# Two-layer hybrid backbone on one core: static buffer rings, a per-feature-tile start for the latent tokens, and modulation vectors spread one per step

## The chip, the cores and the metric

The kernel runs on one core of a Trainium2 chip. The metric is device time in microseconds (us) of one execution, as a median over runs. Five engines work side by side, each through its own list of instructions in order: TensorE (PE, matrix products into PSUM), VectorE (DVE), ScalarE (ACT), GpSimd (POOL) and SyncE (SP, which issues the DMAs). They wait for one another through semaphores.

## What is computed

Two layers of a backbone with 512 latent tokens and 256 context tokens, width 1024, batch 1. The reference, cut to what matters:

```python
def _layer(x, ctx, mod_x, mod_c, lp, rope, update_ctx):
    shift_x, scale_x, gate_x = jnp.split(mod_x[:, None, :], 3, axis=-1)
    shift_c, scale_c, gate_c = jnp.split(mod_c, 3, axis=-1)
    hx = _rms_norm(x, lp['norm_w']) * (1 + scale_x) + shift_x
    hc = _rms_norm(ctx, lp['norm_w']) * (1 + scale_c) + shift_c
    px = _project_stream(hx, lp, rope, True)          # hx @ w_in, split into the branches' parts
    pc = _project_stream(hc, lp, None, update_ctx)
    ya = _dense_attention(...)                        # MLA: latent attention
    yb = _window_attention(...)                       # SWA: window of 128, context, sink
    yc = _dense_attention(...)                        # AXA: axial rope, grouped heads
    yd_x, yd_c = _rglru_branch(...)                   # LRU: gated linear scan in both directions
    x = x + gate_x * _merge_branches((ya, yb, yc, yd_x), px['gate'], px['merge'], lp)
    if update_ctx:
        ctx = ctx + gate_c * _merge_branches(..., pc['gate'], pc['merge'], lp)
    return x, ctx

def _merge_branches(branches, z_gate, z_merge, lp):
    y = jnp.stack(branches, axis=2) * jax.nn.silu(z_gate.reshape(b, n, N_BRANCH, BRANCH_W))
    proj = jnp.einsum('bnkw,kwd->bnkd', y, lp['w_branch'])
    mix = jnp.sum(jax.nn.sigmoid(z_merge.reshape(b, n, N_BRANCH, D_MODEL)) * proj, axis=2)
    return mix @ lp['w_out']

# mod_x = silu(c) @ w_mod[l] + b_mod[l] ; mod_c = silu(c_ctx) @ w_mod[l] + b_mod[l]
```

The modulation vectors (shift, scale and gate, 1024 features each) exist for two conditions: the latent tokens' (condition 0) and the context's (condition 1).

## The kernel before

Activations stand feature by feature: a feature tile is 128 features (partitions) by 768 tokens, the 512 latent ones first. Every operand of a product is split into a high and a low part, and `mm3` (lines 161 to 165) issues three matmuls for each product. Weights come in slots of 128 by 512: `wload` (line 152) issues the DMA into `wraw`, ACT writes the high part `whi` (line 157), POOL the low part `wlo` (line 158). `fgemm` (line 312) makes feature-major products (PSUM tiles `fg`), `tgemm` (line 329) token-major ones for two token tiles (PSUM tiles `tg`). All of it is written as a trace of steps; a scheduler with a timeline of its own then orders the instructions on every engine and places the pools' buffers, so the order on an engine is not that of the source.

**The start.** SP loads the latent x and the first layer's modulation weights (`wmp`, 16 loads of 512 KB, line 180). DVE sums the squares (line 277), PE and POOL make the norm's factor and spread it over the partitions (`rb`, line 292). `scale_pe` (line 190) makes the scales of two feature tiles on PE; `shift2` (line 211) the shift of one feature: condition 0 on DVE (line 213), condition 1 on POOL (product, line 215) and ACT (sum, line 216). `make_hx` (line 298) then writes the normed, modulated feature tile `hx` as a high and a low part: line 302 on DVE, line 304 on ACT, line 305 on DVE. The first product, group `skv` (keys and values of SWA), follows `hx` tile by tile; group `sq` (its queries) comes after it. Then the context's tiles are normed, and the third token pair (context) is projected.

A unit of `gqa_prep` (line 402) is one such product of two token tiles with its tail: values are split (line 399), keys and queries normed and rotated by `head_norm` (line 344: DVE lines 352, 354, 367, 368, 369; POOL lines 341, 342, 365, 366), then transposed by PE and split again (lines 420, 421, 432 to 436).

**The layer.** After SWA's six units and its two gates come SWA's twelve attention pairs (`attn_pair`, line 474; each begins with a row maximum `nm`, line 489, on DVE), with AXA's six units and gates spread between them; then the merge of SWA (m1), AXA's attention with MLA's parts, m2, MLA's attention, the linear recurrence (`lru_scan`, line 726) with the merge of MLA (m3) beside it, the LRU gates `gl`, the merge of LRU (m4) and the output projection (`outproj`, line 836). A merge is eight steps, each with a product `fg`, a tanh on ACT (`mt`, line 812), a branch product `pj`, the product of both on DVE (line 820) and the sum on POOL (line 825). In m4 the sum is also split (`mh` on ACT, line 830, `ml` on DVE, line 831).

**Modulation vectors.** `modvec` (line 247) makes one vector of 128 features: a DMA of 512 KB into `wm`, one multiply-and-sum on DVE for each condition (line 255; the full product goes to a PSUM scrap tile or back into `wm`), then the bias (line 258), and for a scale the gain (line 226) or for a gate a factor 0.25 (line 263). Two calls of `extra()` end each step of m4 and of the output projection, and each takes one vector from a list. In layer 0 that list is filled at m4, with 24 vectors: its own eight gates and the sixteen shifts and scales of layer 1. In layer 1 there are eight, for one condition.

```python
extra()
extra()
if not first:
    pool.tensor_tensor(out=a[:, :N], in0=a[:, :N], in1=t[:, :N], op=ALU.add)
```

## Time and profile before

| | us |
|---|---|
| median of 3 runs | 1443.93 |
| lowest and highest | 1441.81, 1447.64 |
| profiled execution, span (the page gives no other time of that execution) | 1442.5 |
| PE busy | 1358.6 (94%) |
| DVE busy | 916.0 (64%) |
| POOL busy | 733.7 (51%) |
| ACT busy | 672.1 (47%) |

The profile divides one execution by engine, by line and by stretch of time. Its busy time of PE counts a matmul from its issue to its modelled end, and a matmul at the lower of the two clocks as busy for longer, so that idle time and granted clock are read together. A mean granted clock of 1.00 in a stretch is the full 2.4 GHz, 0.50 would be 1.2 GHz throughout.

### The profile page before, as it was taken

What the parts mean: (1) busy time and instruction counts of PE and PEld (TensorE: products, weight loads), DVE (VectorE), ACT (ScalarE), POOL (GpSimd) and SP (SyncE); (2) the same over time, 40 slices, a digit from 0 to 9 for tenths busy, and PEclk for the clock granted to TensorE, in tenths of its full rate; (3) what the DMA queues carried; (4) which work ended last, traced back from release to release, by engine and by line L of the source; (5) the groups of instructions that cost most, each with busy time, mean ns of one, the idle gap of its engine ahead of it and who ended that gap; (6) DMA issues with size and microseconds to landing.
All of it is one profiled execution on the core that took longest, in us unless ns stands there. A gap on an engine that the chain in (4) does not pass through costs nothing. (4 is left out here: it accounts for less than half of the span.)

```text
span 1442.5 us, 22051 instructions
## 1 busy us (share of the span) xinstructions
PE 1358.6 (94%) x8216; PEld 1195.3 (83%) x8216; DVE 916.0 (64%) x1526; ACT 672.1 (47%) x1413; POOL 733.7 (51%) x699
## 2 busy tenths in 40 slices
PE   6699989999999999999978999999999999988998
PEld 4598979899988898888867888999898778876787
DVE  5877875447746755473998367886577476458621
ACT  4445555445545444662222244556455454466231
POOL 4563623223535625675555456554345565468863
PEclk9799999999999999999989999999999999998999
DMA  9021101111111212122453442111221212322534
GB/s 358 29 60 45 40 25 45 52 44 40 46 45 36 61 36 77 52 81 76 167 172 128 155 153 67 52 49 60 67 61 39 73 45 72 98 73 73 162 112 142
DMA packets 58747, 117.82 MB, mean 82 GB/s; under 512 B 6544, under 2 KB 10640, under 8 KB 58640
## 3 DMA queue, kind: packets, MB, share of 16 engines
q1 hardware_dynamic: 58640, 116.42, 25.7%
q8 instruction: 64, 1.05, 0.3%
q14 instruction: 43, 0.35, 0.1%
HBM read 112.20 MB, written 4.19 MB: 81 GB/s over the span
## 5 line engine op out<-in xcount | busy, mean ns | idle before, releaser
L158 POOL TENSOR_TENSOR wlo<-wraw,whi 128x512 fp32r<-128x512 f32 (+2 forms) x298 | 410.4, 1382 | 361.1 <-ACT whi L157 319.6
L163 PE MATMUL fg<-hx,whi 128*128 128x512 f32 x960 | 349.7, 366 | 18.2 <-ACT mt L812 8.8
L164 PE MATMUL fg<-hx,wlo 128*128 128x512 f32 x960 | 348.2, 363 | 8.5 <-POOL wlo L158 8.5
L165 PE MATMUL fg<-hx,whi 128*128 128x512 f32 x960 | 347.1, 362 | 0.0
L157 ACT ACTIVATE whi<-wraw 128x512 fp32r<-128x512 f32 (+2 forms) x298 | 184.7, 621 | 249.3 <-DMA wraw<-in_wall_dram 153.2
L163 PEld LDWEIGHTS fg<-hx,whi 128*128 128x128 f32 x960 | 184.9, 193 | 47.0 <-ACT mt L812 9.8
L164 PEld LDWEIGHTS fg<-hx,wlo 128*128 128x128 f32 x960 | 185.1, 193 | 37.1 <-POOL wlo L158 11.7
L165 PEld LDWEIGHTS fg<-hx,whi 128*128 128x128 f32 x960 | 184.6, 192 | 25.0
L164 PE MATMUL tg<-whi,hx 128*128 128x256 f32 (+1 forms) x528 | 152.1, 290 | 7.5 <-DVE hx L305 7.5
L163 PE MATMUL tg<-whi,hx 128*128 128x256 f32 (+1 forms) x528 | 151.2, 291 | 6.5 <-ACT hx L304 6.4
L165 PE MATMUL tg<-wlo,hx 128*128 128x256 f32 (+1 forms) x528 | 151.0, 289 | 0.6 <-POOL wlo L158 0.5
L523 DVE TENSOR_TENSOR PT<-ptr,PT 128x512 fp32r<-128x512 f32 (+1 forms) x148 | 97.7, 671 | 53.8 <-ACT PT L522 52.4
L496 ACT ACTIVATE P<-s,nm 128x768 f32<-128x768 f32 (+3 forms) x120 | 91.9, 771 | 62.4 <-DVE nm L491 30.5
L522 ACT ACTIVATE PT<-ptr 128x512 fp32r<-128x512 f32 (+1 forms) x148 | 84.2, 584 | 72.9 <-PE ptr L520 67.7
L825 POOL TENSOR_TENSOR acc<-acc,mt 128x768 f32<-128x768 f32 (+1 forms) x48 | 90.1, 1879 | 47.4 <-DVE mt L820 46.4
L164 PEld LDWEIGHTS tg<-whi,hx 128*128 128x128 f32 x528 | 103.6, 197 | 10.1 <-DVE hx L305 9.4
L489 DVE TENSOR_REDUCE nm<-s 128x2 f32<-128x1536 f32 (+3 forms) x60 | 85.9, 1432 | 40.1 <-PE s L165 18.6
L163 PEld LDWEIGHTS tg<-whi,hx 128*128 128x128 f32 x528 | 103.2, 197 | 9.4 <-ACT hx L304 7.4
L165 PEld LDWEIGHTS tg<-wlo,hx 128*128 128x128 f32 x528 | 103.4, 197 | 1.1 <-POOL wlo L158 1.0
L812 ACT ACTIVATE mt<-fg 128x512 f32<-128x512 f32 x96 | 50.1, 522 | 71.9 <-PE fg L165 67.7
L510 DVE TENSOR_SCALAR P<-P,den 128x768 f32<-128x768 f32 (+3 forms) x120 | 80.2, 708 | 2.0
L519 PE MATMUL ptr<-ident,P 128*128 128x128 f32 x288 | 72.1, 278 | 1.8 <-DVE mt L820 1.8
(283 smaller groups left out, 2850.0 us busy)
## 6 DMA issues: line engine op xcount, KB each, us to landing
wraw<-in_wall_dram SPq DMA_DIRECT2D x282, 256.0 KB, 2.6
wm<-in_wmod_dram SPq DMA_DIRECT2D x32, 512.0 KB, 3.2
wmp<-in_wmod_dram SPq DMA_DIRECT2D x16, 512.0 KB, 9.1
x<-in_xT_dram SPq DMA_DIRECT2D x4, 512.0 KB, 6.0
xs<-xn SPq DMA_DIRECT2D x4, 512.0 KB, 3.8
xr<-xs SPq DMA_DIRECT2D x8, 256.0 KB, 2.8
out_dram<-xn SPq DMA_DIRECT2D x4, 512.0 KB, 3.7
wraw<-in_wall_dram SPq DMA_DIRECT2D x8, 160.0 KB, 2.2
```

Of the source, the lines that this page charges most:

```text
L157: act.activation(out=hi[:, :n], in_=raw, func=AF.Copy)
L158: pool.tensor_tensor(out=lo[:, :n], in0=raw, in1=hi[:, :n].bitcast(F32), op=ALU.subtract)
L163: pe.matmul(out=o, lhsT=a[0], rhs=b[0], start=first, stop=False, skip_group_check=True)
L164: pe.matmul(out=o, lhsT=a[1], rhs=b[0], start=False, stop=False, skip_group_check=True)
L165: pe.matmul(out=o, lhsT=a[0], rhs=b[1], start=False, stop=last, skip_group_check=True)
L489: dve.tensor_reduce(out=nm, in_=s3, axis=AX.X, op=ALU.max, negate=True)
L496: act.activation(out=P[i][:, :L], in_=s3[:, i, :], func=AF.Exp, scale=scale, bias=nm[:, i:i + 1], accum_out=den[:, i:i + 1])
L510: dve.tensor_scalar(out=P[i][:, :L], in0=P[i][:, :L], scalar1=den[:, i:i + 1], scalar2=None, op0=ALU.mult)
L519: pe.transpose(tr[:, e * 256:e * 256 + 128], P[0][:, ca:ca + 128], ident)
L522: act.activation(out=q[:, :n], in_=tr[:, :n], func=AF.Copy)
L523: dve.tensor_tensor(out=q[:, 512:512 + n], in0=tr[:, :n], in1=q[:, :n].bitcast(F32), op=ALU.subtract)
L825: pool.tensor_tensor(out=a[:, :N], in0=a[:, :N], in1=t[:, :N], op=ALU.add)
```

## The change

It has four parts. Line numbers of the changed file are given where the prediction needs them.

1. **Rings.** The pools for P, PT, the merge tiles, the raw tiles and the scratch tiles become slices of static tiles that are handed out in turn. P keeps four slices for itself; the merge tiles' ring (three slices) also takes the output projection's residual `xr` and the squares.
2. **The start.** The x loads go first. Only condition 0 is spread at the outset. The latent part of `skv` and of `sq` (four PSUM tiles, `tk`) runs feature tile by feature tile: `first(k)` issues 24 matmuls for tile k. `hx_split` writes the tile with two instructions on ACT and a plain subtraction on DVE (line 322), behind a product x*rb on DVE (line 906). The shifts take the bias as the starting value of the sum (line 239). Everything of the context (`context()`: its eight shifts, now on DVE, its norm and its tiles) stands behind SWA's latent tails, AXA's four latent units come next, then SWA's context units and gates, and AXA's two context units lie between the attention pairs.
3. **Modulation vectors.** Bias, gain and 0.25 go into the multiply-and-sum (line 270), so the small instructions of lines 226, 258 and 263 are gone. One vector per step, and layer 0's list is filled at the scan, so eight vectors lie in m3's steps, eight in m4's and eight in the output projection's.
4. **Wide PSUM tiles.** Every second `fg` of m4 and every second `og` of the output projection uses the three-bank tile `s`.

```diff
-        def g3(name):
-            return sb.tile([128, TOK], F32, name=name, tag="g3", bufs=4)
+        Pt, P_take = ring("P", 4, TOK)
+        PTt, PT_take = ring("PT", 2, 1024, F32R)
+        _, gt_take = ring("gt", 3, TOK)
...
-            dve.tensor_tensor_reduce(out=junk, in0=w, in1=sc[0], scale=1.0, scalar=0.0,
-                                     op0=ALU.mult, op1=ALU.add, accum_out=mod[l][:, f, 0:1])
-            pool.tensor_tensor(out=w, in0=w, in1=sc[1], op=ALU.mult)
-            act.activation(out=w, in_=w, func=AF.Copy, accum_out=mod[l][:, f, 1:2])
+        def shift0(f, i, sc, w, out):
+            dve.tensor_tensor_reduce(out=out, in0=w, in1=sc, scale=1.0, scalar=pv[:, PV_BMOD + f:PV_BMOD + f + 1],
+                                     op0=ALU.mult, op1=ALU.add, accum_out=mod[0][:, f, i:i + 1])
...
+        wm_take = ring("wm", 2, 1024, of=rawt[:, :2048])[1]
+        def modvec(l, f, sc, n=2):
+            w = wm_take()
+            with tc.issue_after(wdma[0].ins):
+                sp.dma_start(out=w, in_=wmod[l, f])
...
             for i in range(n):
+                dve.tensor_tensor_reduce(out=junk if i < n - 1 else w, in0=w, in1=sc[i], scale=sca, scalar=b,
+                                         op0=ALU.mult, op1=ALU.add, accum_out=dst[:, i:i + 1])
...
+        def hx_split(k, i, h, xk):
+            a = dict(in_=xk[:, sl], func=AF.Identity, scale=s1[0][:, k, i:i + 1], bias=mod[0][:, k, i:i + 1])
+            act.activation(out=h[:, 0, sl], **a)
+            act.activation(**{**a, 'out': xk[:, sl]})
+            dve.tensor_tensor(out=h[:, 1, sl], in0=xk[:, sl], in1=h[:, 0, sl].bitcast(F32), op=ALU.subtract)
...
-                z = fgemm(l, ('mrg', b * 8 + f), hx, segs)
+                z = fgemm(l, ('mrg', b * 8 + f), hx, segs, wide("fw") if b == LRU and f % 2 else None)
...
                 extra()
-                extra()
...
+            pts = wide("ow") if f % 2 else None
...
+        px = {('skv', 0): gps("tk"), ('skv', 2): gps("tk"), ('sq', 0): tps("tk"), ('sq', 2): tps("tk")}
+        def first(k):
+            c = (k % 2) * 256
+            for (g, t), p in px.items():
+                w = w0[g][k // 2]
+                for e in range(2):
+                    tk = slice((t + e) * 128, (t + e) * 128 + 128)
+                    mm3(p[:, e * 256:e * 256 + 256], (hx[k][:, 0, tk], hx[k][:, 1, tk]),
+                        (w[0][:, c:c + 256], w[1][:, c:c + 256]), k == 0 and e == 0, k == KT - 1)
+        for c in range(4):
+            for g in w0:
+                w0[g].append(wload(0, (g, c)))
+            if c < 3:
+                wm.append(mod0_load(c + 1))
+            scale_pe(c, scol, wm[c], b1, b2)
+            for k in (2 * c, 2 * c + 1):
+                dve.tensor_tensor(out=xk[k][:, :SEQ], in0=xk[k][:, :SEQ], in1=rb, op=ALU.mult)
+                shift0(k, 0, sc[0], wm[c][2 + k % 2], rawt[:, 1536:2048].bitcast(BF16))
+                hx_split(k, 0, hx[k], xk[k])
+                first(k)
...
+                for (g, t), p in px.items():
+                    sw_post[g == 'sq'](t, p)
+                context()
+                run(ax((0, 2)))
+                run(sw((4,)) + gates(SWA))
+                run(sw_at, ax((4,)) + gates(AXA))
...
+            if l == 0:
+                sc = [cond(scol, i, crow[i]) for i in range(2)]
+                todo += [(0, f) for f in range(16, 24)] + [(1, f) for f in range(16)]
             run(scan, m3[:n4])
```

The order on DVE at three places follows. L numbers are lines of the respective file; of a row, the tile written stands before the arrow.

Place 1, DVE between the latent tiles hx_6, hx_7 and the first tail of SWA (`v0sq`, the split values). Before (L213 is a shift, L305 the low part of hx, L277 a sum of the context's squares, L219 a bias):

```order
L302 SCALAR_TENSOR_TENSOR x_116<-x_116,s_0_99,rb 128x512
L305 SCALAR_TENSOR_TENSOR hx_6_206<-x_116,mod_97,hx_6_206 128x512
L277 TENSOR_TENSOR ssacc<-ssacc,sq 128x256
L305 SCALAR_TENSOR_TENSOR hx_7_207<-x_116,mod_97,hx_7_207 128x512
L277 TENSOR_TENSOR ssacc<-ssacc,sq 128x256 x2
L219 TENSOR_SCALAR mod_97<-mod_97,pvec 128x1
L399 TENSOR_TENSOR v0sq<-tg,v0sq 128x2x64
```

After (L239 a shift with its sum, L322 the low part of hx):

```order
L322 TENSOR_TENSOR hx_6_176<-x_119,hx_6_176 128x512
L322 TENSOR_TENSOR hx_7_177<-x_119,hx_7_177 128x512
L239 ISA wmp_2_127,mod_100<-wmp_2_127,P,consts 128x1024
L239 ISA mod_100 128x1
...
L239 ISA wmp_3_379,mod_100<-wmp_3_379,P,consts 128x1024
L239 ISA mod_100 128x1
L420 TENSOR_TENSOR v0sq<-tk,v0sq 128x2x64
```

The context's eight shifts, which POOL and ACT made before, now stand on DVE between the last latent tile and the first tail.

Place 2, DVE in the linear scan of layer 0 (`lx` are the scan's tiles). Before:

```order
L765 SCALAR_TENSOR_TENSOR lx_00_6352<-lx_00_6352,lx_00_6223 128x768
L761 SCALAR_TENSOR_TENSOR lx_00_6351<-lx_00_6351,lx_00_6223 128x768
L820 SCALAR_TENSOR_TENSOR mt<-mt,pj 128x512
L820 SCALAR_TENSOR_TENSOR mt<-mt,pj 128x256
L762 SCALAR_TENSOR_TENSOR lx_00_6223<-lx_00_6351,lx_00_6223 128x768
L767 SCALAR_TENSOR_TENSOR lx_00_6352<-lx_00_6352,lx_00_6351 128x768
```

After (L270 is a modulation vector's multiply-and-sum):

```order
L785 SCALAR_TENSOR_TENSOR lx_00_6165<-lx_00_6165,lx_00_6012 128x768
L781 SCALAR_TENSOR_TENSOR lx_00_6164<-lx_00_6164,lx_00_6012 128x768
L270 ISA P,mod_100<-raw,P,consts 128x1024
L270 ISA mod_100 128x1
L782 SCALAR_TENSOR_TENSOR lx_00_6012<-lx_00_6164,lx_00_6012 128x768
L840 SCALAR_TENSOR_TENSOR gt<-gt,pj 128x512
L270 ISA raw,mod_100<-raw,P,consts 128x1024
L270 ISA mod_100 128x1
L840 SCALAR_TENSOR_TENSOR gt<-gt,pj 128x256
L787 SCALAR_TENSOR_TENSOR lx_00_6165<-lx_00_6165,lx_00_6164 128x768
```

Vectors now stand between the instructions of the scan and of the merge's steps.

Place 3, DVE in a step of m4 in layer 0. Before:

```order
L820 SCALAR_TENSOR_TENSOR mt<-mt,pj 128x256
L255 ISA junk,mod_98<-wm_2_7836,sc_7217 128x1024
L255 ISA mod_98 128x1
L258 TENSOR_SCALAR mod_98<-mod_98,pvec 128x2
L255 ISA wm_2_7836,mod_98<-wm_2_7836,sc_7230 128x1024
L255 ISA mod_98 128x1
L255 ISA junk,mod_98<-wm_3_7842,sc_7217 128x1024
L255 ISA mod_98 128x1
L258 TENSOR_SCALAR mod_98<-mod_98,pvec 128x2
L831 TENSOR_TENSOR ml_7550<-acc_3008,mh_7549 128x768
L255 ISA wm_3_7842,mod_98<-wm_3_7842,sc_7230 128x1024
L255 ISA mod_98 128x1
```

After:

```order
L840 SCALAR_TENSOR_TENSOR gt<-gt,pj 128x256
L850 TENSOR_TENSOR ml_7133<-acc_2656,mh_7132 128x768
L270 ISA P,mod_101<-raw,P,consts 128x1024
L270 ISA mod_101 128x1
L270 ISA raw,mod_101<-raw,P,consts 128x1024
L270 ISA mod_101 128x1
L840 SCALAR_TENSOR_TENSOR gt<-gt,pj 128x512
L840 SCALAR_TENSOR_TENSOR gt<-gt,pj 128x256
```

Between two merge products there is one vector where there were about two, and no small instruction behind it.

## Rows read from the trace of the kernel before

**Rows 1.** The page: span, and busy time of each engine.

```profile
span 1442.5 us, 22051 instructions
...
PE 1358.6 (94%) x8216; PEld 1195.3 (83%) x8216; DVE 916.0 (64%) x1526; ACT 672.1 (47%) x1413; POOL 733.7 (51%) x699
```

**Rows 2.** Stretches: busy PE, PEld, DVE, ACT, POOL; PE clock; DMA; GB/s.

```profile
20.00:36.00 16.00, 13.94 (x59) 7.41 (x59) 15.08 (x23) 5.62 (x10) 8.19 (x4) 0.79 1.04 398
...
50.00:72.00 22.00, 10.13 (x48) 8.96 (x47) 18.01 (x49) 9.28 (x22) 10.33 (x12) 0.61 0.00 1
```

**Rows 3.** What PE waited for in 0 to 120 us: total, times, longest.

```profile
PE tg L163 <- ACT hx L304: 6.4, 3, 3.8
PE tg L164 <- DVE hx L305: 5.5, 4, 2.6
```

**Rows 4.** DVE by form, 0 to 120 us: busy us, mean ns, idle before.

```profile
L213 DVE CUSTOM_DVE_ANT_0 rb<-wmp,sc 128x1024 f32<-128x1024 f32 x8 | 13.7, 1712 | 2.1 <-PE rb L292 2.0
L305 DVE SCALAR_TENSOR_TENSOR hx<-x,mod,hx 128x512 fp32r<-128x512 f32 x8 | 7.1, 892 | 0.0
L208 DVE SCALAR_TENSOR_TENSOR s<-mod,pvec 128x4 f32<-128x4 f32 x4 | 6.5, 1628 | 0.0
L302 DVE SCALAR_TENSOR_TENSOR x<-x,s,rb 128x512 f32<-128x512 f32 x8 | 5.9, 738 | 0.1
...
L436 DVE TENSOR_TENSOR qT0sq<-qt,qT0sq 64x256 fp32r<-64x256 f32 x6 | 2.6, 427 | 0.1
...
L206 DVE TENSOR_TENSOR mod<-mq,pvec 128x4 f32<-128x4 f32 x4 | 0.6, 150 | 0.0
```

**Rows 5.** POOL by form, 0 to 120 us.

```profile
L215 POOL TENSOR_TENSOR wmp<-wmp,sc 128x1024 f32<-128x1024 f32 x8 | 21.3, 2658 | 17.4 <-DVE mod L213 8.1 <-DVE mod L206 3.6 <-issue 3.5
L158 POOL TENSOR_TENSOR wlo<-wraw,whi 128x512 fp32r<-128x512 f32 x15 | 19.6, 1314 | 22.9 <-ACT whi L157 22.8
```

**Rows 6.** DVE in order of time: start us, us.

```profile
53.44 1.22 DVE L213 CUSTOM_DVE_ANT_0 rb<-wmp,sc 128x1024 f32<-128x1024 f32 x1
...
58.01 0.74 DVE L305 SCALAR_TENSOR_TENSOR hx<-x,mod,hx 128x512 fp32r<-128x512 f32 x1
...
62.41 0.29 DVE L399 TENSOR_TENSOR v0sq<-tg,v0sq 128x128 fp32r<-128x128 f32 x1 [2.74 <-PE tg L165]
...
111.10 1.22 DVE L489 TENSOR_REDUCE nm<-s 128x2 f32<-128x1024 f32 x1
...
216.90 0.68 DVE L489 TENSOR_REDUCE nm<-s 128x2 f32<-128x512 f32 x1
```

**Rows 7.** PE by line, 0 to 82.8 us.

```profile
L164 PE MATMUL tg<-whi,hx 128*128 128x256 f32 x60 | 19.4, 333 | 5.5 <-DVE hx L305 5.5
```

**Rows 8.** PE in order of time, neighbouring matmuls of a unit.

```profile
61.86 0.28 PE L163 MATMUL tg<-whi,hx 128*128 128x256 f32 x1
61.98 0.28 PE L164 MATMUL tg<-whi,hx 128*128 128x256 f32 x1
```

**Rows 9.** Stretches as in rows 2: scan, m3 and m4 of layer 0.

```profile
565.00:660.00 95.00, 90.98 (x507) 79.12 (x506) 55.84 (x50) 50.53 (x76) 60.44 (x40) 0.98 0.21 64
...
700.00:720.00 20.00, 19.35 (x110) 16.63 (x108) 20.00 (x33) 3.39 (x6) 10.89 (x5) 1.00 0.45 155
720.00:740.00 20.00, 15.40 (x76) 12.66 (x75) 19.89 (x27) 5.39 (x10) 13.21 (x6) 0.91 0.53 178
740.00:760.00 20.00, 16.79 (x75) 13.65 (x74) 20.00 (x30) 3.91 (x7) 9.21 (x6) 0.83 0.45 155
...
780.00:800.00 20.00, 15.97 (x83) 13.81 (x83) 9.25 (x13) 6.14 (x12) 9.75 (x7) 0.91 0.30 94
```

**Rows 10.** DVE by form, 695 to 800 us.

```profile
L255 DVE CUSTOM_DVE_ANT_0 junk<-wm,sc 128x1024 f32<-128x1024 f32 x20 | 29.3, 1464 | 0.1
...
L258 DVE TENSOR_SCALAR mod<-mod,pvec 128x2 f32<-128x2 f32 x21 | 13.4, 639 | 0.0
```

**Rows 11.** Stretch as in rows 2: m4 of layer 1.

```profile
1339.00:1365.00 26.00, 23.10 (x91) 17.73 (x90) 18.20 (x37) 6.80 (x12) 20.84 (x13) 0.93 0.60 198
```

More of the change, by code (lines that the diff above doesn't have):

```diff
@@ L147, in consts @@
             dve.tensor_scalar(out=hb, in0=pv[:, PV_BR:PV_BR + 16], scalar1=0.5, scalar2=None, op0=ALU.mult)
+            for l in range(DEPTH):
+                b = pv[:, PV_BMOD + 24 * l + 16:PV_BMOD + 24 * l + 24]
+                dve.tensor_scalar(out=b, in0=b, scalar1=0.25, scalar2=None, op0=ALU.mult)
+            b = pv[:, PV_BMOD + 32:PV_BMOD + 40]
+            dve.scalar_tensor_tensor(out=b, in0=b, scalar=1.0, in1=pv[:, PV_NORM + 8:PV_NORM + 16],
+                                     op0=ALU.add, op1=ALU.mult)
         wdma = [None]
@@ L180, in mod0_load @@
         def mod0_load(c):
-            mk = big if c != 1 else (lambda n: sb.tile([128, 2, TOK], F32, name=n, tag="hx", bufs=8))
-            ws = [mk(f"wmp{c}_{q}").rearrange("p a b -> p (a b)")[:, :1024] for q in range(4)]
+            ws = [sb.tile([128, 1024], F32, name=f"wmp{c}_{q}", tag="wq", bufs=12) for q in range(4)]
             for q in range(2):
@@ L230, in cond @@
-        def cond(scol, mk, n=2):
-            ts = []
-            for i in range(n):
-                t = mk(f"sc{i}")
-                for e in range(2):
-                    p = gps("scb")
-                    for k in range(4):
-                        c = 2 * (4 * e + k) + i
-                        pe.matmul(out=p[:, k * 128:k * 128 + 128], lhsT=scol[:, c:c + 1].to_broadcast([128, 128]),
-                                  rhs=ident, start=True, stop=True, skip_group_check=True)
-                    act.activation(out=t[:, e * 512:e * 512 + 512], in_=p, func=AF.Copy)
-                ts.append(t)
-            return ts
@@ new lines, in scale_pe, with cond @@
+            dve.scalar_tensor_tensor(out=s1[0][:, 2 * c:2 * c + 2, :], in0=mod[0][:, f:f + 2, :], scalar=1.0,
+                                     in1=col(PV_NORM + 2 * c), op0=ALU.add, op1=ALU.mult)
+        def shift0(f, i, sc, w, out):
+            dve.tensor_tensor_reduce(out=out, in0=w, in1=sc, scale=1.0, scalar=pv[:, PV_BMOD + f:PV_BMOD + f + 1],
+                                     op0=ALU.mult, op1=ALU.add, accum_out=mod[0][:, f, i:i + 1])
+        def cond(scol, i, t, ps_=None):
+            for e in range(2):
+                p = gps("scb") if ps_ is None else ps_[e]
+                for k in range(4):
+                    c = 2 * (4 * e + k) + i
+                    pe.matmul(out=p[:, k * 128:k * 128 + 128], lhsT=scol[:, c:c + 1].to_broadcast([128, 128]),
+                              rhs=ident, start=True, stop=True, skip_group_check=True)
+                act.activation(out=t[:, e * 512:e * 512 + 512], in_=p, func=AF.Copy)
+            return t
@@ L371, in raw_tile @@
         def raw_tile(name):
-            return tp.tile([128, 512], F32, name=name, tag="raw", bufs=3)
+            return raw_take()
         tails = []
@@ L572, in step @@
                 gqa_attn(j, t, qT, kT, v, y, br == SWA, ns, sk)
-            return prep, [lambda j=j, t=t: step(j, t) for j in range(2) for t in qtiles]
+            return prep, post, [lambda j=j, t=t: step(j, t) for j in range(2) for t in qtiles]
         def mla_c(l, hx, qtiles):
@@ L878, in body @@
[L878 to L889 removed]
+        b0, b1, b2 = rbs[:, 0:512], rbs[:, 512:1024], rbs[:, 1024:1536]
@@ new lines, in body, with context @@
+        for kp in range(4):
+            sp.dma_start(out=xt[kp][:, :, SEQ:], in_=xT[kp][:, :, SEQ:])
+        def context():
+            sc.append(cond(scol, 1, crow[1], (b0, b2)))
+            for k in range(KT):
+                shift0(k, 1, sc[1], wm[k // 2][2 + k % 2], wm[k // 2][2 + k % 2])
+            state = {}
+            for k in range(KT):
+                sumsq(xk[k][:, SEQ:], k, state)
+            rb = rstd_bcast(state, CTX, b0[:, :256], b2)
+            for k in range(KT):
+                dve.tensor_tensor(out=xk[k][:, SEQ:], in0=xk[k][:, SEQ:], in1=rb, op=ALU.mult)
+                hx_split(k, 1, hx[k], xk[k])
@@ L952, in body @@
             m4 = branch(LRU)
-            if l == 0:
-                sc = cond(scol, row)
-                todo += [(0, f) for f in range(16, 24)] + [(1, f) for f in range(16)]
-            else:
-                sc = cond(scol, row, 1)
+            if l == 1:
+                sc = [cond(scol, 0, crow[0])]
                 todo += [(1, f) for f in range(16, 24)]
```

220 lines of the change are left out of this document (98 added, 122 removed).

## The prediction, made before the changed kernel was run

> **What bounds the kernel now.** I read the page first. PE is busy for 94% of the span, DVE for 64% [rows 1]. The products do not change in number, so the time can only fall by what PE loses: stretches in which it waits, or works at a granted clock below 1.00. I looked for these with the table of stretches, then asked the waits of PE and the forms on DVE in each.
>
> Two places stand out. One is the start. From 20 to 36 us the DMAs run without a break at 398 GB/s, and from 50 to 72 PE is busy for only 10.1 of 22 us, at a mean clock of 0.61, while DVE is busy for 18.0 [rows 2]. PE waits there for the feature tiles: 6.4 us for their high part on ACT, 5.5 for the low part on DVE [rows 3]. So DVE sets the pace. The other is m4 of layer 0: from 700 to 760 us DVE is busy for 59.9 of 60 us, PE for 51.5, with the clock at 0.91 and 0.83 in two of the three stretches [rows 9]. DVE's time there goes into modulation vectors: 20 of them from 695 to 800 us, with 1.46 us for the first sum of each and 0.64 for its bias [rows 10].
>
> **The start, step by step.** On DVE between the norm's factor and the last latent tile stand 13.7 us of shifts, 5.9 of x times scale and factor, 7.1 of low parts, 6.5 and 0.6 of scales: 33.8 us [rows 4]. Much of it is waiting. A scale of 128x4 takes 1.63 us on average where its neighbour of the same size takes 0.15, and a shift 1.71 where the undisturbed one takes 1.22 [rows 4, 6]; POOL's eight products for the context (2.66 us each) [rows 5] run beside them. The change takes those products away from POOL. What is left on DVE: 8 shifts at 1.22 and 0.14 for reading the sum (10.9), 8 times x*rb at 0.74, 8 subtractions at 0.74 (the undisturbed low part) [rows 6], 8 small ones at 0.15: 23.9 us. That would end tile 7 ten us sooner, but the loads stand against it. x, modulation and the first two groups' weights are 12 MB in all, 30 us at 398 GB/s, from about 7 us on; the last shift's weights then land near 37 us. Behind that lie two shifts, two x*rb, four subtractions and a scale that goes through PE and ACT. Followed by hand through the new order that gives 52 us for tile 7 (bounds 46 and 58), against 58.7 before [rows 6].
>
> PE then has the products of both groups done at 52 + 24 x 0.12 = 55 us (0.12 us apart) [rows 8]. Before, 180 of the 192 were issued by 82.8 us (60 of each kind) [rows 7], since `sq` began only after `skv`. So PE has a **head start of 27 us**.
>
> I expect most of it to be given back. Place 1 of the order shows why: eight context shifts, 10.9 us, stand on DVE ahead of the first tail. It begins at 63, where it began at 62.4 before [rows 6]. PE cannot run ahead without limit, since its next units need the PSUM tiles that still hold these sums. And DVE has more to do ahead of the first row maximum: besides the shifts, the tails of AXA's four latent units. These are 20 norm instructions (half of them 512 columns wide at 0.74 us, half at about half of that: 11 us), some 20 split pieces at 0.43 [rows 4], value splits and a gate: 20 us. The first row maximum was at 111.1 [rows 6], 48.7 us behind the first tail; now it is 49 + 20 behind it, less some of the 10 us that DVE stood idle: about 128 (bounds 120 and 142). By then PE has 97 more products of units (11.6 us) and one more gate (24 matmuls of 512 columns and 24 of 256, 8.5 us) behind it, in 17 us more: a gain of **3 us**. That is the term I am least sure of. Its ends are the full head start, +27, and the loss of the fourth rival below, -34; I take 3 because the rows of DVE, from which it comes, are the nearest to this work. Two small things ride on it: the squares and norm of the context are the same instructions, later; the softplus chain comes out of the constants but stays on DVE before the first row maximum.
>
> **m4 of layer 0.** Lost there: from 700 to 760 us PE is idle for 8.5 us, and runs 15.4 us at 0.91 and 16.8 at 0.83, which is 4.3 us of work not done; from 780 to 800 it is 4.0 idle and 1.4 by the clock [rows 9]. After, a step has one vector instead of two and no small instructions. In these 60 us DVE did about 11 vectors, at 2 x 1.46 for the sums, 0.2 for reading them, 0.64 for the bias and as much again for gain or factor: 48 of the 60 us. Half as many without the small ones are 5.5 x 3.1 = 17, so DVE needs 29 us where PE needs 47. PE becomes the bound, and the first 12.8 us return; of the 5.4 behind 780, where DVE is busy for less than half, I count half. **15.5 us**, bounds 10 and 18.
>
> **The eight vectors that move to the scan.** Each is 3.1 us on DVE and one DMA of 512 KB on SP's queue, which waits for the ring slot that the vector two before it used; weights queue behind it there. DVE is busy for 55.8 of 95 us from 565 to 660 [rows 9]; 25 more make 81. It fits, but place 2 shows vectors inside the scan's chain, so the scan ends later, and m4's branch products wait for it. At worst all of the eight stand in the chain with nothing beside (25 us less the idle 39: below zero), at best none does. I take **-2 us**, bounds 0 and -6.
>
> **Layer 1's m4.** PE is idle for 2.9 of 26 us and loses 1.6 by the clock [rows 11]. One vector per step instead of two: half comes back, **2.5 us** (0 to 4.5).
>
> **Wide PSUM tiles and rings.** A third pair of banks lets PE begin a product before the tanh has emptied the last. It can return only what is left of the waits around m4 and the projection: the other half of 5.4 us. I take **1.5** (0 to 2.7). The rings hand out as many buffers as the pools did, except that squares, `xr` and merge tiles share three; the cover is POOL's and DVE's slack in the projection, and without it a step would wait for one square, under 1 us. I cost it at nothing.
>
> Sum: 3 + 15.5 - 2 + 2.5 + 1.5 = 20.5 us. The profiled span of 1442.5 becomes 1422; the median of the runs stands 1.4 above that span, so **1423**.
>
> **A rule of the Trainium skill** bears on the moved shifts. The rows show a DVE instruction stretched while POOL works: 1.63 us against 0.15, 1.71 against 1.22 [rows 4, 6]. I price a moved shift as undisturbed, because POOL's products are gone. The Trainium skill (SBUF — State Buffer, Who interferes with whom) says that a DVE instruction with two inputs in SBUF and a GpSimd instruction that reads SBUF lock each other out for the whole instruction. By that rule, with which the stretched scale agrees, the move itself is no cure, since POOL's low parts of the weights read SBUF too.
>
> **Rivals.**
> 1. *The start keeps its head start.* PE's tails find DVE free, and the waits for tiles [rows 3] do not come back. For it: POOL's interference goes. Against it: DVE's added 31 us ahead of the first row maximum. Between half of the 27 us and all of it: 1412 down to 1399.
> 2. *DVE is stretched by POOL's weights.* A low part takes 1.31 us [rows 5]; if each of the eight context shifts waits for one, the first tail comes 10.5 us later, and PE with it: 1423 + 10.5 = 1434. For it: the stretched rows. Against it: it takes a low part beside each of the eight. (The rule of the Trainium skill named above is this mechanism.)
> 3. *The stall is only moved.* The eight vectors hold the scan back as they held m4 (the 25 us come through in place of 2 by more than half, 15 us), and the start gives nothing: 1443.9 - 20.5 + 15 + 3 = 1441, no change. The DVE sum of 81 in 95 us speaks against it; the chain of the scan for it.
> 4. *Slower: SWA's attention runs without cover.* Before, its twelve pairs lay from 111.1 to 216.9 us [rows 6], 9.6 us each, with six AXA units (6 x 48 x 0.12 = 34.6 us of products) between them. Now only two units are left there (11.5 us). If a pair's chain through DVE, ACT and POOL needs its 9.6 us whatever PE does, 23 us of PE's time have no work. If the first row maximum comes at 142 instead of 128 as well, another 14 are lost. Then the start costs 34 instead of giving 3: 1423 + 37 = 1460, and with half of it 1442. It decides from a first row maximum at about 140. For it: the missing units. Against it: DVE has those units' tails behind it by then, so the chain is shorter.
>
> **How the numbers follow.** Forecast (within about 10 us of 1423): 0.58. Rival 1: 0.17. Rival 2: 0.10. Rival 3: 0.08. Rival 4: 0.07. A difference of 0.5% (7.2 us) is about what a measurement of this kernel can tell from no change: faster is below 1436.7, slower above 1451.1. Faster: nearly all of the forecast, rival 1, and two thirds of rival 2: 0.81. Slower: most of rival 4, with a little of rival 3: 0.06. The rest, 0.13, is the same. The range takes in the forecast, the milder half of rival 1, rival 2 and some of rival 3: 1404 to 1439.
>
> **What would show it.** Right: tile 7's low part near 52 us, the first value split near 63, the first row maximum near 128; PE busy without a gap in m4 with DVE at about 60%; no wait of `fg` for the tanh there. Wrong: PE's work at 130 us ahead of before by more than 10 us (rival 1), moved shifts over 2 us (rival 2), PE idle in the scan or before the LRU merge's branch products (rival 3), PE idle between SWA's pairs (rival 4).

## The result, and the profile after

The changed kernel takes **1462.4 us** (median of 4 runs), the kernel before took 1445.8 on the same chip: ratio 1.0127, interval 1.0107 to 1.0148. The forecast of 1423 and its range were wrong; the change made the kernel slower by 16.6 us. The page of after, to be read against [rows 1]:

```profile
span 1459.5 us, 22114 instructions
...
PE 1358.1 (93%) x8216; PEld 1192.2 (82%) x8216; DVE 909.1 (62%) x1473; ACT 683.9 (47%) x1429; POOL 737.2 (51%) x707
```

PE's work is the same; the span is 17 us longer. The stretches of after, in the columns of [rows 2] (the first two and 740 to 760 answer to [rows 2, 9]):

```profile
20.00:36.00 16.00, 14.02 (x76) 8.15 (x74) 10.11 (x18) 5.12 (x10) 2.63 (x2) 1.00 1.05 395
50.00:72.00 22.00, 19.94 (x137) 16.27 (x136) 12.79 (x18) 11.55 (x23) 7.76 (x6) 0.92 0.23 66
65.00:90.00 25.00, 16.92 (x139) 16.51 (x138) 18.52 (x34) 6.08 (x15) 12.33 (x14) 0.96 0.10 31
90.00:112.00 22.00, 8.93 (x40) 8.19 (x41) 17.65 (x31) 8.55 (x24) 11.31 (x11) 0.51 0.17 48
112.00:140.00 28.00, 19.86 (x136) 18.63 (x135) 22.38 (x60) 14.97 (x30) 17.39 (x18) 0.86 0.18 51
...
740.00:760.00 20.00, 20.00 (x117) 17.66 (x116) 8.84 (x13) 6.08 (x10) 9.19 (x8) 1.00 0.39 119
```

Of before, from 65 to 112 us:

```profile
65.00:90.00 25.00, 21.65 (x149) 20.86 (x150) 20.87 (x59) 9.58 (x21) 14.34 (x17) 0.80 0.14 43
90.00:112.00 22.00, 19.54 (x137) 17.51 (x136) 15.62 (x23) 10.85 (x24) 14.89 (x14) 1.00 0.24 64
```

Two things can be read at once. In m4 PE is now busy without a gap at a granted clock of 1.00, which was the aim. And from 90 to 112 us it is busy for 8.9 of 22 us, where before had 19.5. To see where time went, I counted PE's work matmul by matmul (each at its undisturbed distance to the next) and compared when both kernels had done the same amount. After is 24 us behind where before stood at 125 us, 17 at 217, 28 at 552, 33 at 660 (behind the scan); m4 brings that to 11 at 808; the passage to layer 1 makes it 16 at 918; then it is 13 at 1217, 23 at 1245 in the second scan, and 16 at 1366 behind the second m4. So the start loses, then a stretch between 217 and 552, both scans and the passage, and the two m4 gain.

PE's longest waits of after from 0 to 170 us:

```profile
PE kt L438 <- DVE raw L432: 22.3, 3, 11.3
PE rb L291 <- DVE P L284: 4.1, 1, 4.1
PE rb L248 <- DVE scol L206: 3.4, 1, 3.4
PE rb L224 <- DVE x L906: 3.0, 2, 1.5
```

`kt` are the transposes of SWA's keys. They wait for L432, DVE's copy that doubles the normed keys; before, PE's only such wait took 0.8 us:

```profile
PE kt L417 <- DVE kdup L411: 0.8, 1, 0.8
```

DVE of after in order of time (L233 adds the bias to a scale):

```profile
58.66 0.16 DVE L233 TENSOR_TENSOR mod<-rb,consts 128x4 f32<-128x4 f32 x1 [3.76 <-PE rb L229]
...
63.21 1.88 DVE L322 TENSOR_TENSOR hx<-x,hx 128x512 fp32r<-128x512 f32 x2 [3.12 <-ACT x L321]
65.54 1.28 DVE L239 CUSTOM_DVE_ANT_0 wmp<-wmp,P,consts 128x1024 f32<-128x1024 f32 x1 [0.45 <-ACT P L250]
...
77.24 0.28 DVE L420 TENSOR_TENSOR v0sq<-tk,v0sq 128x128 fp32r<-128x128 f32 x1
...
93.52 0.41 DVE L432 COPY raw<-raw 128x512 f32<-128x512 f32 x1
...
101.52 0.43 DVE L432 COPY raw<-raw 128x512 f32<-128x512 f32 x1
...
170.13 1.23 DVE L509 TENSOR_REDUCE nm<-s 128x2 f32<-128x1024 f32 x1
```

The low parts of tiles 6 and 7 are written from 63.2 to 65.1 (forecast for tile 7: 52), the first value split begins at 77.2 (63; before 62.4), the first row maximum at 170.1 (128; before 111.1) [rows 6]. Of ACT, the norm's squares (L371) and the evacuations of a query unit (L470) in the same place:

```profile
80.73 0.42 ACT L371 ACTIVATE raw<-raw 128x256 f32<-128x256 f32 x1 [2.04 <-DVE raw L389]
84.64 0.63 ACT L371 ACTIVATE raw<-raw 128x512 f32<-128x512 f32 x1 [3.49 <-DVE raw L389]
94.02 0.60 ACT L470 ACTIVATE raw<-tk 128x512 f32<-128x512 f32 x1 [7.72 <-DVE raw L432]
```

The squares of one unit wait until DVE has added the rotation of the unit before (L389), and the fourth unit's evacuation waits 7.7 us for the first doubled keys.

### The profile page after: what moved, and what is told of

It reads as the page before. It is cut to its first block, busy times and chain, and to the rows that moved or that the text cites. A ratio compares the mean times of both kernels' runs of the same rounds, so it can differ in the third digit from the quotient of the medians.

```text
span 1459.5 us, 22114 instructions
## 1 busy us (share of the span) xinstructions
PE 1358.1 (93%) x8216; PEld 1192.2 (82%) x8216; DVE 909.1 (62%) x1473; ACT 683.9 (47%) x1429; POOL 737.2 (51%) x707
## 4 chain that ended last, share of the span: by engine, by line
PE 36%; POOL 6%; DVE 4%; issue 4%; DMA 2%; ACT 2%; SPq 0%; POOLq 0%; ACTq 0%
PE fg L193 5%; PE fg L192 5%; PE fg L194 5%; POOL wlo L187 3%; DMA wraw<-in_wall_dram 2%; PE pvo L546 2%; PE tg L194 1%; PE tg L193 1%; PE tg L192 1%; PE s L566 1%; PE fw L192 1%; PE fw L193 1%; PE fw L194 1%; PE pj L193 1%; PE pj L192 1%
## 5 line engine op out<-in xcount | busy, mean ns | idle before, releaser
L187 POOL TENSOR_TENSOR wlo<-wraw,whi 128x512 fp32r<-128x512 f32 (+2 forms) x314 | 438.1, 1399 | 402.7 <-ACT whi L186 380.5
L193 PE MATMUL fg<-hx,wlo 128*128 128x512 f32 (+1 forms) x864 | 311.0, 360 | 8.6 <-POOL wlo L187 8.6
L192 PE MATMUL fg<-hx,whi 128*128 128x512 f32 (+1 forms) x864 | 310.7, 362 | 7.5 <-ACT whi L186 5.8
L194 PE MATMUL fg<-hx,whi 128*128 128x512 f32 (+1 forms) x864 | 310.0, 360 | 0.0
L193 PEld LDWEIGHTS fg<-hx,wlo 128*128 128x128 f32 x864 | 164.7, 191 | 34.2 <-POOL wlo L187 12.4
L192 PEld LDWEIGHTS fg<-hx,whi 128*128 128x128 f32 x864 | 164.3, 191 | 31.6 <-ACT whi L186 7.1
L194 PEld LDWEIGHTS fg<-hx,whi 128*128 128x128 f32 x864 | 164.5, 190 | 22.1
L192 PE MATMUL tg<-whi,hx 128*128 128x256 f32 (+1 forms) x464 | 134.0, 291 | 4.9 <-DVE v0aq L420 2.1
L193 PE MATMUL tg<-whi,hx 128*128 128x256 f32 (+1 forms) x464 | 133.6, 290 | 4.0 <-DVE hx L322 1.9
L194 PE MATMUL tg<-wlo,hx 128*128 128x256 f32 (+1 forms) x464 | 132.8, 290 | 2.6 <-POOL wlo L187 2.6
L844 POOL TENSOR_TENSOR acc<-acc,gt 128x768 f32<-128x768 f32 (+1 forms) x48 | 83.1, 1732 | 27.9 <-DVE gt L840 19.0
L192 PEld LDWEIGHTS tg<-whi,hx 128*128 128x128 f32 x464 | 91.3, 197 | 6.4 <-DVE v0aq L420 2.5
L193 PEld LDWEIGHTS tg<-whi,hx 128*128 128x128 f32 x464 | 91.2, 197 | 5.9 <-DVE hx L312 3.0
L832 ACT ACTIVATE gt<-fg 128x512 f32<-128x512 f32 x84 | 43.7, 523 | 71.8 <-PE fg L194 69.1
```

The source lines that it names most:

```text
L187: pool.tensor_tensor(out=lo[:, :n], in0=raw, in1=hi[:, :n].bitcast(F32), op=ALU.subtract)
L192: pe.matmul(out=o, lhsT=a[0], rhs=b[0], start=first, stop=False, skip_group_check=True)
L193: pe.matmul(out=o, lhsT=a[1], rhs=b[0], start=False, stop=False, skip_group_check=True)
L194: pe.matmul(out=o, lhsT=a[0], rhs=b[1], start=False, stop=last, skip_group_check=True)
```

## The experiments

All kernels compute the whole result. The quoted texts were written before each run and number the theories in the order in which they came up; the lines ahead of each say what is asked. Ratios are to the kernel before, with their interval.

**Which part loses.** e3 takes back the start and the order of units alone, keeping rings, spread vectors and wide tiles.

```diff
-        sc = [cond(scol, 0, crow[0], (b1, b2))]
+        sc = [cond(scol, i, crow[i]) for i in range(2)]
...
+                shift2(k, wm[c][2 + k % 2])
+                with tc.high_priority():
+                    shift_bias(k, 0)
+                    make_hx(0, k, 0, hx[k], xk[k], rb)
...
+            run(sw(PAIRS))
+            run(gates(SWA))
+            run(sw_at, ax(PAIRS) + gates(AXA))
```

> The changed kernel with the start and the order of units of the kernel before: both conditions at the outset, the second on GpSimd and ScalarE, SWA's six units, then its attention with AXA's six. Rings, folded and spread modulation and wide PSUM tiles stay. If the start holds the loss (the work curve of PE puts it at 16 to 19 us up to the end of SWA's attention): 1443 to 1447. If the rings hold it: about 1460. If the other parts bring what was forecast for them (17.5 us): 1426.

Measured 1442.5 us, 0.9997 (0.9987 to 1.0008). The start loses 20 us against e3, and all the other parts together are worth nothing, which the forecast had at 17.5. By the count of PE's work e3 is 7 us behind already at 125 us (with PE's waits for the doubled keys at 4.8 us), loses 7 in the scan and as much in the passage, and gains 22 in m4. e4 takes back the spreading alone: the list is filled at m4, two vectors a step.

```diff
-            if l == 0:
-                todo += [(0, f) for f in range(16, 24)] + [(1, f) for f in range(16)]
             run(scan, m3[:n4])
...
                 extra()
+                extra()
```

> The changed kernel, but layer 0's modulation vectors begin at m4 again, two per step, and two per step of the projection; bias, gain and factor stay folded in. If the spreading brought m4's gain (22 us on the work curve) and cost the scan 7 and the transition between the layers 5: m4 becomes bound by DVE again for part of it, 1457 to 1467. If the folding alone brought the gain: scan and transition get their 12 us back, about 1450.

Measured 1476.1, 1.0226 (1.0208 to 1.0244): 13.7 us slower than after, and above both ranges. The stretch of m4, bounded by the count so that it holds the same work of PE in each kernel (before, e4, after):

```profile
700.00:808.00 108.00, 94.58 (x496) 80.34 (x494) 92.20 (x136) 24.98 (x45) 54.10 (x28) 0.94 0.44 149
733.70:830.70 97.00, 90.80 (x495) 78.01 (x494) 87.73 (x103) 24.65 (x44) 53.70 (x28) 0.96 0.55 173
732.20:818.10 85.90, 85.90 (x495) 75.90 (x494) 42.91 (x61) 25.33 (x43) 42.11 (x27) 1.00 0.45 139
```

So with two folded vectors per step m4 already takes 11 us less than before, and one per step takes another 11 off: both changes have their half of the gain. By the count the scan of e4 loses no less than that of after (11 and 8 us from 545 to 660, and 10 each in layer 1), so the vectors are not its cause. e7 is e3 without the wide tiles (`None` for both).

> The kernel with the old start (1442.5 us), but without the wide PSUM tiles. If they bring what was forecast (1.5 us): 1443 to 1445. If they let m4 run without a gap (m4's gain of 22 us was 6 above the forecast): 1447 to 1450. If they cost the projection and the transition between the layers 7 us: 1436 to 1439.

Measured 1452.4, 1.0060 (1.0041 to 1.0079): 9.9 us slower than e3 (9 by the ratios), where I had 1.5 for the wide tiles. By the count none of it lies in layer 0 (both 2 us ahead at 862 us), and some 6 of it in layer 1's m3, which uses no wide tile: there PE waits longer for POOL's low parts of the weights. So taking the tiles out also moved the order elsewhere, and 9.9 is not the price of the tiles alone.

**The scan.** The trace of after shows SP's queue from 575 to 620 us (what each DMA issue waited for: total, times, longest):

```profile
SPq L183 <- POOL PT L753: 25.0, 2, 23.3
SPq L183 <- POOL wlo L187: 19.9, 8, 6.7
```

L753 is POOL's low part of the scan's own gate weights. The rings put their raw weights into `wraw`, the ring of two that every weight load uses, and both parts of them into slices of PT, which MLA's attention still reads. ACT's high part (L752) can only begin behind one of its products (`pvo`):

```profile
587.93 0.63 ACT L752 ACTIVATE PT<-wraw 128x512 fp32r<-128x512 f32 x1 [4.88 <-PE pvo L546]
```

Until then both slots are held, and loads of the merge wait 23 us. e6 gives them a slice of scratch in e3:

```diff
-                raw = wp.tile([128, 512], F32, name="wraw", tag="wr", bufs=2)
+                raw = sb_take()
```

> The kernel with the old start (1442.5 us), but the scan's gate weights are loaded into a scratch slice of their own instead of the ring of the projections' weights. Theory 4 (part of the 7 us that the scan of layer 0 loses, and of the 9 in layer 1, is that these loads hold the weight ring while the attention still reads the tiles that they are split into; it shows without the spreading too): the losses at the beginning of both scans go, 1432 to 1438. Rival (the vectors in the scan cost it): no change, 1441 to 1444.

Measured 1432.0, 0.9919 (0.9905 to 0.9934): 10.5 us from one line (11 by the ratios); by the count of PE's work neither scan of e6 loses anything against before. In e6 from 545 to 600 us no weight load waits for it any more:

```profile
SPq L183 <- POOL wlo L187: 39.9, 9, 11.6
SPq L753 <- POOL PT L755: 3.6, 1, 3.6
```

e11 takes the projection's residual out of the merge ring as well:

```diff
-                xr = gt_take()
+                xr = big(f"xr{l}{f}{which[0]}")[:, 0, :]
```

> The best kernel so far (old start, scan weights apart, 1432 us), but the output projection's residual gets tiles of its own instead of the three-slot ring that it shares with the squares. If this sharing costs the 6 us between the end of m4 and layer 1's first units (they are lost with and without the wide tiles, and with and without the spreading): 1425 to 1428. If not: 1431 to 1434.

Measured 1428.4, 0.9889 (0.9866 to 0.9913): some 4 us more, though the intervals of e6 and e11 overlap.

**The start: why is tile 7 late?** DVE waits for the scale of a pair of tiles (the row at 58.66 above), and PE, which makes it, waits in the row `rb L224 <- DVE x L906`: the scale rows now stand in the PSUM tile whose first bank holds the norm's factor, and their products wait until DVE has read that other bank, since the program orders accesses by tile. e1 gives the rows a bank of their own.

```diff
         def scale_pe(c, scol, ws, p, pm):
+            p = pv_.tile([128, 256], F32, name="mrp", tag="pv")
```

> The changed kernel, but the rows of the scales get a PSUM bank of their own; before they shared one three-bank tile with the spread norm factor, and each group's scale products waited for the x*rb of the group before. Theory 1 (this wait paces the start): tile 7's low part comes at about 55 us instead of 65, the first value split at about 67 instead of 77, and the time falls by 7 to 10 us from 1462. Theory 2 (DVE's work behind the tiles paces it, the context's shifts and the tails): tile 7 comes sooner, but the first row maximum does not, and the time falls by less than 3 us.

Measured 1455.3, 1.0086 (1.0071 to 1.0101): about 7 us back (by the ratios, 6). PE's wait for L906 is gone. Tile 7 is written from 52.1 and the first value split begins at 63.5, both as forecast; but the first row maximum only comes at 167.0, and PE waits 24.1 us for the doubled keys. So the head start was there, and was lost again.

**Are the context's shifts in the way?** e2 holds them until the norms of SWA's latent tails are issued.

```diff
+            with tc.issue_after(hn_last[0].ins):
                 for k in range(KT):
                     shift0(k, 1, sc[1], wm[k // 2][2 + k % 2], wm[k // 2][2 + k % 2])
```

> The changed kernel, but the context's eight shifts stand on DVE behind the norms of SWA's latent tails instead of ahead of them. Theory 2 (the shifts ahead of the tails hold PE at the key transposes): the first value split comes at about 69 us instead of 77, PE's 18 us of waiting for the doubled keys fall below 8, and the time falls by 8 to 12 us from 1462. Theory 1, or if the shifts only move on to hold the context instead: the waits for the keys shrink, but the time falls by less than 4 us.

Measured 1461.3, 1.0118 (1.0100 to 1.0136), no gain: the first split comes at 67.8, the first row maximum at 168.4, and PE's waits for the doubled keys only fall to 17.4 us. e9 does them early, in DVE's idle time before tile 7 (both conditions at the outset, ten `wmp` slots for twelve), and e10 adds the bank of e1.

```diff
-        sc = [cond(scol, 0, crow[0], (b1, b2))]
+        sc = [cond(scol, i, crow[i], (b1, b2)) for i in range(2)]
...
                 first(k)
+                shift0(k, 1, sc[1], wm[c][2 + k % 2], wm[c][2 + k % 2])
```

> The changed kernel, but both conditions are spread at the outset and the context's eight shifts are made on DVE beside the latent ones (ten buffers instead of twelve for the modulation weights). Theory 5 (DVE paces everything up to SWA's attention, and the change left it idle for 22 of the 45 us from 20 to 65, where it idled for 4 before; work put back there is taken off the path): the first row maximum comes 8 to 12 us before 170, and the time falls by 8 to 11 us from 1461. Rival (the round trips of the tails between DVE, GpSimd and ScalarE pace it, not DVE's work): the first value split comes at about 68 us, but the first row maximum moves by less than 4 us, and so does the time.

> The run before this one, and the scales' rows in a PSUM bank of their own. Theory 5: the tiles also come 10 us sooner, 1440 to 1447. Rival: as the own bank alone, 1452 to 1456.

Measured 1455.7, 1.0076 (1.0050 to 1.0101), and 1454.3, 1.0072 (1.0044 to 1.0100): 6 to 8 us, not added up. e12 is e10 with the scan's weights apart.

> The kernel of two runs before (early shifts, own bank) and the scan weights apart. If the scan's loss is independent of the start, as the work curve of PE says: 10 to 11 us below that kernel.

Measured 1445.9, 1.0002 (0.9987 to 1.0017), 14 us above e6 (12 by the ratios): most of the start's loss is still there.

**Do AXA's units come too early?** e5 puts them back between the attention pairs, e8 does so with the bank of e1.

```diff
                 context()
-                run(ax((0, 2)))
                 run(sw((4,)) + gates(SWA))
-                run(sw_at, ax((4,)) + gates(AXA))
+                run(sw_at, ax(PAIRS) + gates(AXA))
```

> The changed kernel, but AXA's four latent units go back between SWA's attention pairs; the per-feature-tile start and the later context stay. Theory 3 (the first row maximum, at 170 us instead of 111, waits for DVE, which has AXA's tails as well as the context ahead of it, and PE idles behind it): the first row maximum comes at 135 to 150 us and the time falls by 8 to 15 us from 1461. Rival (AXA's units cover the making of the context, and without them PE waits for the context's tiles instead): the first row maximum comes sooner, PE idles before SWA's context units, and the time changes by less than 4 us.

> The changed kernel with both: the scales' rows in a PSUM bank of their own, and AXA's units back between the pairs. If the chain of the scales and DVE's work ahead of the first row maximum are the two costs of the start, they add up: 7 us from the first and 8 to 15 from the second, 1440 to 1447. If only one of them ends last, the sum is no lower than the better of the two, 1447 to 1455.

Measured 1461.2, 1.0123 (1.0108 to 1.0138), and 1468.1, 1.0175 (1.0158 to 1.0192). The first row maximum of e5 comes at 130.5, 40 us earlier, and the time stays. Its stretches tell why:

```profile
65.00:90.00 25.00, 5.16 (x44) 4.96 (x42) 18.50 (x34) 5.06 (x13) 12.30 (x14) 0.67 0.11 31
90.00:112.00 22.00, 7.20 (x28) 5.86 (x28) 15.44 (x37) 9.06 (x23) 6.00 (x7) 0.50 0.00 0
```

PE is busy for 12.4 us of 47. AXA's units were the cover of the tails, not their obstacle, and the first row maximum is no measure of the start. e8 missed both of its ranges: by the count it is 3 us ahead of e5 up to 862 us, and loses that and more in the passage and in layer 1, which its edit does not touch. So the order elsewhere can move a total by some us.

**What the tails wait for.** In e10, with tile 7's products done and the shifts out of the way, ACT's rows still read as those of after:

```profile
77.03 0.42 ACT L371 ACTIVATE raw<-raw 128x256 f32<-128x256 f32 x1 [3.55 <-DVE raw L389]
80.97 0.63 ACT L371 ACTIVATE raw<-raw 128x512 f32<-128x512 f32 x1 [3.51 <-DVE raw L389]
88.34 0.60 ACT L470 ACTIVATE raw<-tk 128x512 f32<-128x512 f32 x1 [1.48 <-DVE raw L432]
```

Every norm uses one scratch slice for the squares and the first rotation product, another for the second product and the doubled keys. Four units now end together and queue for them. e13 gives each ring a second slice and the raw ring a fourth, from the P ring, which is idle until the attention; e14 does so in e12, and e16 in e12 without the fourth raw slice.

```diff
-        _, sa_take = ring("sa", 1, 512, of=rawt[:, 1536:2048])
-        _, sb_take = ring("sb", 1, 512, of=rawt[:, 2048:])
+        sa_take = more([3], [0])
+        sb_take = more([4], [1])
+        raw_take = more([0, 1, 2], [5])
...
+                spare[0] = False
                 run(sw((4,)) + gates(SWA))
```

Here `more` hands out slices of `rawt` (first list) and, while `spare[0]` holds, of the P ring (second list), in turn.

> The changed kernel, with a second slice for each of the norm's two scratch rings (squares and first rotation product; second rotation product and doubled keys) and a fourth raw slot, all in the idle P ring, until the context units of SWA. Theory 6 (the four latent tails end together and then queue for one scratch slice; before, the products came 6 us or more apart): PE's waits for the doubled keys fall from 23.2 us to under 15, first row maximum 170 to about 155, time 1462 to 1448-1456. Theory 7 (PE only lacks other work while each tail's chain through DVE, ACT and POOL runs; scratch is not what it waits for): waits and time as in the changed kernel, 1459-1464.

> The same second slices and fourth raw slot, put into the kernel with both conditions at the outset, scale rows in their own bank and scan weights apart (1446 us, first row maximum about 154). Theory 6: the squares of a unit no longer wait 3.5 us for the rotation of the one before, the fourth raw evacuation no longer waits for the doubled keys; PE's waits for the doubled keys fall from 12.3 us to under 6, first row maximum to about 140, time 1433-1440. Theory 7: 1443-1448.

> As the kernel before it, with the second scratch slices alone and three raw slots. Theory 6: between the two, as the fourth raw evacuation still waits for the first doubled keys: 1437-1444. If scratch alone is the limit, the same as with the fourth slot. Theory 7: 1443-1448.

Measured: e13 1441.7, 0.9980 (0.9964 to 0.9995), **20.7 us faster than after**; e14 1430.5, 0.9906 (0.9881 to 0.9931), 15.5 faster than e12 (14 by the ratios); e16 1433.1, 0.9911 (0.9882 to 0.9939), 13 faster than e12 by the ratios, so nearly all of it comes from the scratch pair. All three gain more than theory 6 had. By the count 13 us of e13's gain stand at 217 us; 6 more come up to 450, where the second slices are no longer handed out, and their cause is open. In e14 ACT no longer waits for a rotation (L393 are the squares, L492 the query evacuations):

```profile
72.42 0.45 ACT L393 ACTIVATE raw<-raw 128x256 f32<-128x256 f32 x1
...
73.25 0.63 ACT L492 ACTIVATE raw<-tk 128x512 f32<-128x512 f32 x1
73.88 0.69 ACT L393 ACTIVATE raw<-P 128x512 f32<-128x512 f32 x1
75.32 0.63 ACT L393 ACTIVATE raw<-raw 128x512 f32<-128x512 f32 x1 [0.75 <-DVE hn_ss L395]
```

PE's waits for the doubled keys fall from 12.3 us (e12) to 3.6:

```profile
PE kt L460 <- DVE P L454: 2.3, 2, 1.7
PE kt L460 <- DVE raw L454: 1.3, 1, 1.3
```

**Is that a limit of the new order alone?** e17 is e13 with the bank of e1, the scan's weights and the residual apart; e18 is e11 (the old start) with the second pair of scratch slices.

> The changed kernel with all that the runs point to, its start's order kept: second scratch slices and fourth raw slot, scale rows in their own bank, the scan's gate weights and the residual out of the shared rings. By theory 6 the parts add: 1442 (scratch) - 10 (scan weights) - 4 (residual) - 0 to 3 (bank) = 1425-1428, so that the order of the changed start is then as good as the old one (1428). If the start's order itself were worse, this would stay 5 us or more above 1428: 1433-1440.

> Control for theory 6: the second scratch slices (squares, rotation, doubled keys) in the kernel with the start of before, scan weights and residual apart (1428 us). There the products of two units end 6 us or more apart, so the scratch is not what the tails wait for: 1426-1429, a gain of 0 to 2 us. If the second slices brought 8 us or more here too (1420 or less), the single scratch was simply a limit of both kernels and not what made the change slower.

Measured: e17 1430.3, 0.9900 (0.9882 to 0.9918), between its two ranges; e18 **1418.4, 0.9820 (0.9801 to 0.9838)**, the fastest of all. The control went against me: the old start gains 10.0 us too, where I expected 0 to 2. By the text put down ahead of it, the single pair was a limit of both kernels. In e11 ACT's query evacuations (L472) had waited for the doubled keys too (first row); in e18 they do not, and PE's stretch from 90 to 140 us closes (second row e11, third row e18):

```profile
ACT raw L472 <- DVE raw L434: 10.1, 2, 5.5
90.00:140.00 50.00, 44.23 (x298) 40.22 (x297) 30.59 (x54) 20.30 (x50) 24.30 (x26) 0.93 0.15 43
90.00:140.00 50.00, 50.00 (x379) 47.37 (x378) 34.31 (x62) 25.45 (x62) 28.31 (x34) 1.00 0.18 49
```

What these buffers explain of the start's loss is therefore only the difference: the new order lay 20 us behind the old (after and e3), and with all four mended it still lies 12 behind (e17 and e18). DVE of e17 shows a part of these 12 (L261 is a shift of the context):

```profile
68.07 1.28 DVE L261 CUSTOM_DVE_ANT_0 wmp<-wmp,P,consts 128x1024 f32<-128x1024 f32 x1 [0.20 <-ACT P L272]
...
70.49 2.31 DVE L261 CUSTOM_DVE_ANT_0 wmp<-wmp,P,consts 128x1024 f32<-128x1024 f32 x1
...
88.88 0.42 DVE L454 COPY P<-raw 128x512 f32<-128x512 f32 x1
```

The eight shifts stand inside the tails, and the first doubled keys come 25 us behind the first split (63.2). But the shifts are not all of it. From 90 to 140 us (first row e17, second row e14, whose shifts are early) PE is busy for 37.8 and 37.5 of 50 us:

```profile
90.00:140.00 50.00, 37.82 (x230) 35.22 (x229) 46.13 (x113) 29.08 (x71) 29.77 (x32) 0.74 0.15 45
90.00:140.00 50.00, 37.53 (x244) 35.34 (x245) 43.77 (x103) 28.75 (x67) 33.27 (x33) 0.80 0.24 66
```

By the count e17 is 10 us ahead of e18 at 65 us, 17 behind at 125 and 11 behind at 217: most of the 12 us is lost there, ahead of the first pair. DVE is busy for 46.1 and 43.8 of these 50 us, and for 34.3 in e18, so its work ahead of the pairs is the next suspect; no run takes it apart.

## Why the prediction was wrong

By its own steps:

- **The start, +3 us: measured -20** (after against e3). This step failed, and it makes 23 of the 37 us between the forecast change (-20.5) and the measured one (+16.6). Two of its sentences were wrong. "Followed by hand through the new order that gives 52 us for tile 7": it was 65, because PE's rows of scales share a PSUM tile with the norm's factor, and I followed the rows of the order without asking what each instruction waits for; e1 gives back 52, and some 7 us of time. "Now it is 49 + 20 behind it": I priced the four tails by what DVE has to do and left out what they hand to each other. One slice of scratch serves all; while it is held, DVE is idle as well (18.5 of 25 us busy from 65 to 90 us). The row maximum came 93 us behind the first split, not 65 to 69. A second pair of slices gives back 20.7 us, but gives the old start 10 as well. Against the old order, mending the scratch, the bank and the rings brings the loss from 20 us to 12 (e17 and e18); what makes these 12, most of them lost from 90 to 140 us, stays open.
- **m4 of layer 0, +15.5: measured about 22** (33 us behind at 660, 11 at 808). Right in mechanism and place; PE is busy for 85.9 of 85.9 us. The term was too small by 6 us: by the count 6 us come back behind 780 us, where I had taken half of 5.4, and 16 up to there, where I had 12.8.
- **Eight vectors in the scan, -2: the scan lost 5 to 8 (from 552 or from 545 us on), and 10 in layer 1, but not through them.** Without spreading (e4) it lost no less.
- **Rings, "at nothing": 10.5 us** for the scan's weights in the weight ring and some 4 for the residual in the merge ring. This step failed. I counted slots and did not ask for how long each is held: both slots of a two-slot ring were held while the DMA queue waited 23 us.
- **Layer 1's m4, +2.5: 6** (22 us behind at 1339, 16 at 1366); half of the 4.5 us would have been 2.3. **Wide tiles, +1.5: up to 9.9** (e7), all in layer 1; I had looked for their price in PE's waits of layer 0.

Of the rivals, the slower one (1442 to 1460) named the right size, and its sign, a first row maximum behind 140, came. But PE did not run out of work among SWA's pairs, which lie from 170 to 260 us in after:

```profile
170.00:260.00 90.00, 88.17 (x665) 81.99 (x664) 64.82 (x124) 52.70 (x147) 39.78 (x62) 1.00 0.19 55
```

PE had no work before the first pair, in front of the key transposes. Rival 2 was a small part: two of the context's eight shifts took 2.3 us instead of 1.28. Rival 3 found a stall moved to the scan, with a different cause.

Along the count of PE's work: 28 lost up to 552 us (20 of them by the start's order, the rest in e3 as well; 10 of the 20 only between 217 and 552, for a reason that stays open), 5 in the scan, 22 gained in m4, 6 lost in the passage, 4 gained up to 1217, 10 lost in the second scan, 6 gained in the second m4: 17 slower, as the runs say.

## What to carry to other kernels

When several units are made to end together, ask first which buffer their tails share: price a tail by the chain through its scratch as well as by the busy time of an engine, and try the same buffer in the old order before calling it the cause. When pools become rings, list for each slot what frees it and how long that takes; one slow holder in a two-slot ring stops the DMA queue behind it. And where a regrouping brings the expected gain at one place (m4), undo the other parts one by one before judging it: here 44 us lay between the change (1462.4) and its good parts on the old start with three buffers added (1418.4).

## What the runs showed of the hardware

A DVE and a POOL instruction that both read SBUF stretched each other. In e17 POOL's low part of a weight and one of DVE's shifts overlap, and both take about 1 us longer than alone (2.22 against 1.27, 2.31 against 1.28):

```profile
69.28 1.28 DVE L261 CUSTOM_DVE_ANT_0 wmp<-wmp,P,consts 128x1024 f32<-128x1024 f32 x1
69.49 2.22 POOL L209 TENSOR_TENSOR wlo<-wraw,whi 128x512 fp32r<-128x512 f32 x1
...
80.61 1.27 POOL L209 TENSOR_TENSOR wlo<-wraw,whi 128x512 fp32r<-128x512 f32 x1 [1.26 <-ACT whi L208]
```

POOL's product begins beside the shift of 69.28 and ends 1.2 us behind that shift's end; the next shift (70.49) ends 1.1 us behind POOL's product. Each thus took about its own time once the other was done. That agrees with the rule of the Trainium skill (SBUF — State Buffer, Who interferes with whom) that the prediction quoted. Its price over the eight shifts of after was 2 us (two took 2.3), not the 10.5 of rival 2, since only those shifts pay that meet such a product; in e17 three took 2.3.
